# Three late modulation rows: features on partitions and a row sum on VectorE

## The chip, the cores and the metric

The kernel runs on one core of a Trainium2 chip. The metric is the device time of one execution in microseconds (us), lower is better. Of three runs the median was 1469.58 us (1468.6 to 1469.86).

## The reference, cut to what matters

One layer of a hybrid backbone: two adaLN modulated inputs (256 latent tokens `x`, 256 context tokens), one input projection, three mixers (S5, convolution, mLSTM), an output projection, then a SwiGLU FFN. Only this part of it is touched:

```python
def _adaln(c_vec, w_mod, b_mod):                # D_MODEL = 2048, w_mod (2048, 6*2048)
    m = jax.nn.silu(c_vec) @ w_mod + b_mod
    return jnp.split(m[..., None, :], 6, axis=-1)
sh1_x, sc1_x, g1_x, sh2_x, sc2_x, g2_x = _adaln(c, w_mod[l], b_mod[l])
x = x + g1_x * (jnp.concatenate([s5_x, cv_x, ml_x], axis=-1) @ w_out[l])
hx2 = _rmsnorm(x, norm2_g[l]) * (1.0 + sc2_x) + sh2_x
x = x + g2_x * _swiglu(hx2, w_ffn_in[l], w_ffn_out[l])
```

`sh1` and `sc1` are needed first and are formed elsewhere. The four later rows are called q = 0 (`g1`), 1 (`sh2`), 2 (`sc2`) and 3 (`g2`). Each is a product of a 2048 vector with a 2048 x 2048 fp32 matrix of 16 MB.

## The kernel before, in words

**The main stream.** All large weights lie in HBM in the order of use, as chunks of eight 128 x 128 tiles (512 KB). SP fetches chunk c into `raw` (L259, three buffers), ScalarE rounds it to `whi` (L201) and VectorE forms the rest `wlo = raw - whi` (L168). TensorE then runs three fp32r matmuls per tile (`mm3`, all recorded at L208), with 256 tokens as columns. `nxt()` hands out tiles and starts the fetch and the split one or two chunks ahead.

**The stages, by time in the profiled execution.** The first modulation rows and the first tiles of the input projection (to 150 us), the rest of the projection with convolution, S5 and k (to 350), v (to 443), q and o with attention (to 582), the gate of S5 and the output projection in two halves (to 691), the second norm and the first four FFN column blocks (`make_h2`, to 744), the FFN (to 1455), the final norm.

**The four late rows.** `wm_dma` (L331) loads pieces of 128 x 1024 fp32 (512 KB) on POOL's queue into four buffers `wm`; the first four before the job starts, and one more for each piece used. `mod_job` (L719) walks q, then four column blocks b of 512 features, then 8 pieces. For q = 0 TensorE multiplies each piece with the vector `cs`. For q = 1 to 3, the three rows that the change touches, the piece has model inputs on partitions: ScalarE writes the first scaled step into `macc` (L195), VectorE adds 15 further steps, each a SCALAR_TENSOR_TENSOR of 128 x 512 (L179) with one column of `cs` as its scalar. The sum over the 128 partitions is still open. Four TensorE transposes (L749) put the features on partitions and ScalarE adds each along its row (L755, with an accumulator read). `macc` has one buffer, so the next block cannot begin before L755 is through with it.

**What sets the order.** `Sched` is a planner with modelled clocks of TensorE, VectorE and ScalarE. Its `pump()`, called at every chunk, lets jobs emit code: a job that yields n waits n ns of modelled TensorE time, here 5000 for each piece (`MOD_PACE_D`; 4000 for q = 3), and nothing is emitted while the modelled VectorE or ScalarE is over 3500 ns ahead. `mst["go"]` holds q = 1 back until the k stage and q = 3 until the first FFN blocks are emitted. `need_mod(q)` emits what is left when a row is needed: q = 0 before the output projection, q = 2 after its first half (L1178), q = 3 before the first FFN output (L1274). The text order is then a priority only: when the program is built, a scheduler may put an instruction on its engine ahead of the text where its inputs and its buffer are free, unless the text pins it (`keep_in_program_order`, as for the ScalarE step of q = 3 at L738). On the chip every engine and every DMA queue takes its instructions in the order so fixed.

Of the kernel before, what the change touches and what calls it, by code (L numbers as in the profile page):

```python
# [10 lines left out]
F32 = mybir.dt.float32  # L11
F32R = mybir.dt.float32r
I32 = mybir.dt.int32
AF = mybir.ActivationFunctionType
OP = mybir.AluOpType
# [4 lines left out]
KT = 16  # L20
# [14 lines left out]
MOD_PACE = 3200.0  # L35
MOD_PACE_F = 4000.0
MOD_PACE_D = 5000.0
# [5 lines left out]
CONV_STEP = 2  # L43
GO_AT = {'k': 2}
LEAD_R, LEAD_S = 2, 1
MOD_PE = {(0, b) for b in range(4)}

# [98 lines left out]


@with_exitstack  # L150
def hybrid_layer_kernel(ctx: ExitStack, tc: tile.TileContext, xt, ctxt, wm1, wmr, wst, wg, bvrow, pvd, cstd, s5p, out):
    nc = tc.nc
    V, S, P, G = nc.vector, nc.scalar, nc.tensor, nc.gpsimd
    sb = ctx.enter_context(tc.tile_pool(name="sb", bufs=1))
# [3 lines left out]
    sc = Sched()  # L158


    def n_of(ap):
        n = 1
        for s in ap.shape[1:]:
            n *= s
        return n

    def tt(o, a, b, op):
        V.tensor_tensor(out=o, in0=a, in1=b, op=op)  # L168
        sc.dve += 62 + 1.05 * n_of(o)

    def ts(o, a, s1, op0, s2=None, op1=None):
        if op1 is None:
            V.tensor_scalar(o, a, s1, None, op0=op0)
        else:
            V.tensor_scalar(o, a, s1, s2, op0=op0, op1=op1)
        sc.dve += 62 + 0.6 * n_of(o)

    def stt(o, a, s, b, op0, op1):
        V.scalar_tensor_tensor(o, a, s, b, op0=op0, op1=op1)  # L179
        sc.dve += 62 + 1.05 * n_of(o)  # L180

    def vcopy(o, a):
# [3 lines left out]
    def rsum(o, a):  # L186
        V.tensor_reduce(out=o, in_=a, op=OP.add, axis=mybir.AxisListType.X)
        sc.dve += 62 + 1.05 * n_of(a)
# [5 lines left out]
    def act(o, a, f, bias=0.0, scale=1.0, pin=False):  # L194
        i = S.activation(o, a, f, bias=bias, scale=scale)  # L195
        if pin:
            tc.keep_in_program_order(i)
        sc.act += 190 + 0.84 * n_of(o)

    def acopy(o, a):  # L200
        S.copy(o, a)  # L201
        sc.act += 190 + 0.84 * n_of(o)

    def mm(o, l, r, start, stop, native=False, tp=None, sgc=False, pin=False):
        kw = {}
        if tp is not None:
            kw["tile_position"] = tp
        i = P.matmul(o, lhsT=l, rhs=r, start=start, stop=stop, skip_group_check=sgc, **kw)  # L208
        if pin:
            tc.keep_in_program_order(i)  # L210
        n = n_of(o)
        sc.pe += (max(n * 4, 512) if native else max(n, 256)) / 2.36 / (1 if tp is None else 4)

    def bank(tag, bufs, dt=F32):
        return pp.tile([128, 512], dt, name="ps_" + tag, tag=tag, bufs=bufs)

    def mbank():
        return bank("m", 3)

    def qbank():  # L220
        return bank("qk", 2)

    def bbank():
        return bank("b", 3)

    def tmp(n=512):
        return sb.tile([128, 512], F32, name="tmp", tag="tmp", bufs=4)[:, :n]
# [9 lines left out]
    def pvc(name, i=0, n=None):  # L237
        a, w = PV[name]
        return pv[:, a + i:a + i + (n if n is not None else 1)]
# [77 lines left out]
    wm = {}  # L317
# [7 lines left out]
    def wm_dma(key, src, q=None):  # L325
        slot = (4 * key[0] + key[1]) % NWX if len(key) == 2 else 0
        if slot < NWM:
            wm[key] = sb.tile([128, 1024], F32, name="wm", tag="wm", bufs=NWM)
        else:
            wm[key] = wm_extra[slot - NWM]  # L330
        i = (q or nc.gpsimd).dma_start(wm[key], src)  # L331
        if q is not None:
            tc.keep_in_program_order(i)
# [33 lines left out]

    plan_pump()

    cs = sb.tile([128, KT, 32], F32, name="cs")  # L370
    V.memset(cs, 0.0)
    act(cs[:, :, 0], pvc("c", 0, 16), AF.Silu)
    act(cs[:, :, 1], pvc("cc", 0, 16), AF.Silu)
    b1sc = sb.tile([128, 16], F32, name="b1sc")
    ts(b1sc, pvc("bm", 16, 16), 1.0, OP.add)

    hx = sb.tile([128, KT, 2, NT], F32R, name="hx", tag="hx")
# [29 lines left out]
    for half, src in ((0, xr), (1, cr)):  # L407
        for q in range(4):
# [4 lines left out]
            for i in range(2):  # L413
                mm(stp[:, half * 256:half * 256 + 256], ones, sq[:, 256 * i:256 * i + 256], q + i == 0, q + i == 4,
                   native=True)
# [288 lines left out]

    mods = sb.tile([128, 4, 16], F32, name="mods")

    mq = [(q, b, kp) for q in range(4) for b in range(4) for kp in range(8)]
    mst = {"d": 0, "q": 0, "go": 0}

    def phase(n):  # L710
# [2 lines left out]
    def mod_dma():  # L713
        if mst["d"] < len(mq):
            i = mq[mst["d"]]
            wm_dma(i, wmr[i[0], i[1], i[2]])
            mst["d"] += 1

    def mod_job():  # L719
      for q in range(4):  # L720
        while mst["go"] < q:
            yield 500
        for b in range(4):
            on_pe = (q, b) in MOD_PE
            acc = sb.tile([128, 512], F32, name="macc", tag="macc", bufs=1)
            if on_pe:
                psm = bbank()
            for kp in range(0, 8, 2):
                w = [wm.pop((q, b, kp + i)).rearrange("p (k n) -> p k n", k=2) for i in range(2)]
                for j in range(4):  # L730
                    kt = 2 * kp + j
                    wj = w[j // 2][:, j % 2, :]
                    s = cs[:, kt, 0:1]
                    if on_pe:
                        mm(psm[32 * j:32 * j + 32, :], cs[:, kt, :], wj, kt < 4, kt >= 12, native=True, tp=(0, 32 * j),
                           pin=j > 0)
                    elif kt == 0:
                        act(acc, wj, AF.Copy, scale=s, pin=q == 3)  # L738
                    else:
                        stt(acc, wj, s, acc, OP.mult, OP.add)  # L740
                mod_dma()
                mod_dma()
                yield 2 * (MOD_PACE if on_pe else MOD_PACE_D if q < 3 else MOD_PACE_F)
            dst = mods[:, q, 4 * b:4 * b + 4]
            if on_pe:
                acopy(acc, psm)
            ps = bbank()
            for j in range(4):
                P.transpose(ps[:, 128 * j:128 * j + 128], acc[:, 128 * j:128 * j + 128], ident)  # L749
                sc.pe += 110  # L750
            if on_pe:
                rsum(dst, ps.rearrange("p (f j r) -> p f j r", f=4, j=4)[:, :, :, 0])
            else:
                for j in range(4):
                    S.activation(acc[:, 128 * j:128 * j + 128], ps[:, 128 * j:128 * j + 128], AF.Copy,  # L755
                                    accum_out=dst[:, j:j + 1])
                    sc.act += 390
            tt(dst, dst, pvc("bm", 32 + 16 * q + 4 * b, 4), OP.add)
            yield
        mst["q"] = q + 1  # L760

    def need_mod(q):
        mst["go"] = max(mst["go"], q)
# [169 lines left out]
    for t in range(4):  # L933
        ps = mbank() if t else bbank()
# [68 lines left out]
    for ct in range(KHEAD, 8):  # L1003
        ps = mbank()
        for kt in range(KT):
            w = nxt()
# [116 lines left out]
    for ct in range(8):  # L1123
        ps = mbank()
# [3 lines left out]
    for ct in range(8):  # L1128
        ps = mbank()
# [31 lines left out]
    for ct in range(4):  # L1161
        ps = mbank()
        for kt in range(4):
            mm3(ps[:, 0:256], nxt(), (gs[:, kt, 0, :], gs[:, kt, 1, :]), kt == 0, kt == 3)
        sg, f = tmp(256), tmp(256)
# [5 lines left out]
    for ct in range(KT):  # L1171
        ps = mbank()
        for i in range(8):
            src, j = (mx["c"], i) if i < 4 else (mixs, i - 4)
# [38 lines left out]
    for ct in range(KT):  # L1213
        ps = mbank()
# [32 lines left out]
    def ffn_in(b):  # L1247
        ffa = (ffp if b % 2 else sb).tile([128, FBLK, 2, NT], F32R, name="ffa", tag="fb" if b % 2 else "hx")
        ffas[b] = ffa
        i0 = 0  # L1250
        if b == 0:
            pss = [mbank(), mbank(), mbank(), qbank()]
            for kt in range(KT):
                make_h2(kt)
                hh = (h2[:, kt, 0, :], h2[:, kt, 1, :])
                for i in range(FHEAD):
                    mm3(pss[i][:, 0:256], nxt(), hh, kt == 0, kt == KT - 1, sgc=True)
                    mm3(pss[i][:, 256:512], nxt(), hh, False, kt == KT - 1, sgc=True)
            for i in range(FHEAD):
                swiglu(ffa, i, pss[i])  # L1260
            i0 = FHEAD
            mst["go"] = 3
        for i in range(i0, FBLK):
            ps = bbank() if b == 0 and i < FHEAD + 2 else mbank()
            fourA(1, h2, ps[:, 0:256])
            fourA(1, h2, ps[:, 256:512])
            swiglu(ffa, i, ps)

    s3 = None
    for kind, b in FSEQ:  # L1270
# [8 lines left out]
        for ct in range(KT):  # L1279
            ps = mbank()  # L1280
# [13 lines left out]
    i = 0  # L1294
# [8 lines left out]
def pack(inp):  # L1303
    f = {k: np.asarray(v) for k, v in inp.items()}
# [7 lines left out]
    a = {}  # L1312
    a["xt"] = feat(f["x"][0])
    a["ctxt"] = feat(f["ctx"][0])
    wmod = f["w_mod"][0]
    m1 = wmod[:, :4096].reshape(4, 4, 128, 2, KT, 128)
    a["wm1"] = np.ascontiguousarray(m1.transpose(4, 0, 2, 1, 3, 5)).reshape(KT, 4, 128, 1024)
    mr = wmod[:, 4096:].reshape(8, 2, 128, 4, 4, 512)
    a["wmr"] = np.ascontiguousarray(mr.transpose(3, 4, 0, 2, 1, 5)).reshape(4, 4, 8, 128, 1024)
    mats = {"in": f["w_in"][0][:, :OFF_G], "out": f["w_out"][0], "glu": f["s5_w_glu"][0], "ffi": f["w_ffn_in"][0],  # L1320
            "ffo": f["w_ffn_out"][0]}
    til = {k: m.reshape(m.shape[0] // 128, 128, m.shape[1] // 128, 128) for k, m in mats.items()}
    w = np.empty((NCH, 128, CH, 128), np.float32)
# [49 lines left out]
    for r in range(32):  # L1373
        q = r % 16
# [9 lines left out]
    return a  # L1384


_INS = ["xt", "ctxt", "wm1", "wmr", "wst", "wg", "bvrow", "pvd", "cstd", "s5p"]


# [19 lines left out]
```

## Time and profile before

| | us |
|---|---|
| median of three runs | 1469.58 |
| the profiled execution, device time | 1469.76 |
| its span, first to last instruction | 1468.0 |
| TensorE busy | 1423.0 (97%) |
| VectorE busy | 1004.2 (68%) |
| ScalarE busy | 716.0 (49%) |
| bytes moved by DMA | 315.56 MB, mean 215 GB/s |

The device time is 1.76 us more than the span. An engine that is busy for most of the span may still wait for another one in some stage, so the rows below go by stage. A matmul's shown duration overlaps the next one's; the distance between starts is what a matmul takes of the time.

### The profile page before, as it was taken

To read this page: it belongs to the slowest core of one execution; us is meant where nothing else is said; L and a number is where in the kernel's file an instruction comes from. 1 tells how busy PE (TensorE), PEld (TensorE's weight loads), DVE (VectorE), ACT (ScalarE), POOL (GpSimd) and SP (SyncE) were. 2 spreads that over 40 slices of the span, in tenths; PEclk is the share of its full clock that TensorE was granted. 3 is DMA by queue.
4 is the path that set the end of the run, shared out by engine and by line. 5 is a ranking of instruction groups with operands and counts; after the bars stand their busy time and mean duration, and the time that the engine had idled before them with its cause. 6 is when DMAs were issued, how large, how long until landed. Compare 5 with 4: busy or idle time off the path is not lost.

```text
span 1468.0 us, 29243 instructions
## 1 busy us (share of the span) xinstructions
PE 1423.0 (97%) x11840; PEld 1335.7 (91%) x11840; DVE 1004.2 (68%) x1960; ACT 716.0 (49%) x1199; POOL 107.2 (7%) x207
## 2 busy tenths in 40 slices
PE   6999899999999999998999999999999999999996
PEld 3888788887878999998999999999999999999996
DVE  7655699998988787988776667555544554555554
ACT  4333786654656555545544444433444334443353
POOL 1221111110101011111010000000000000000000
PEclk9999999999999999999999999999999999999999
DMA  9997464443436576688477786555555555555553
GB/s 359 360 360 294 160 234 138 165 162 123 147 121 233 196 270 237 239 312 321 150 262 269 257 291 237 186 187 187 185 184 185 186 188 182 186 187 187 186 175 114
DMA packets 87943, 315.56 MB, mean 215 GB/s; under 512 B 10096, under 2 KB 10880, under 8 KB 87808
## 3 DMA queue, kind: packets, MB, share of 16 engines
q1 hardware_dynamic: 60912, 216.67, 42.9%
q0 software_dynamic: 26896, 97.02, 18.4%
q8 instruction: 93, 1.52, 0.4%
q14 instruction: 42, 0.34, 0.1%
HBM read 311.55 MB, written 2.10 MB: 214 GB/s over the span
## 4 chain that ended last, share of the span: by engine, by line
PE 87%; DVE 4%; ACT 3%; DMA 2%; issue 2%; SPq 0%; POOL 0%; DVEq 0%; POOLq 0%; ACTq 0%
PE ps_m L208 71%; PE ps_b L208 11%; PE ps_qk L208 4%; DMA wm<-in_wm_dram 1%; DVE tmp L168 1%; DMA tmp<-in_wg_dram 1%; DVE macc L179 1%; DMA raw<-in_wst_dram 1%; DVE wlo L168 1%; PE ps_b L839 0%; ACT whi L201 0%; ACT tmp L195 0%; ACT U L201 0%; PE ps_b L749 0%; DVE xres L168 0%
## 5 line engine op out<-in xcount | busy, mean ns | idle before, releaser
L168 DVE TENSOR_TENSOR wlo<-raw,whi 128x1024 fp32r<-128x1024 f32 x386 | 471.9, 1224 | 315.9 <-ACT whi L201 311.1
L201 ACT CAST whi<-raw 128x1024 fp32r<-128x1024 f32 x386 | 404.0, 1047 | 502.3 <-PE ps_m L208 355.9
L208 PE MATMUL ps_m<-h,whi 128*128 128x256 f32 x2624 | 469.9, 282 | 3.6 <-ACT h L195 3.6
L208 PEld LDWEIGHTS ps_m<-h,whi 128*128 128x128 f32 x2624 | 403.8, 189 | 4.0 <-ACT h L195 4.0
L208 PE MATMUL ps_m<-h,wlo 128*128 128x256 f32 x1312 | 369.6, 282 | 0.0
L208 PE MATMUL ps_m<-ffa,whi 128*128 128x256 f32 x1408 | 251.1, 281 | 0.0
L208 PEld LDWEIGHTS ps_m<-h,wlo 128*128 128x128 f32 x1312 | 247.5, 189 | 0.0
L208 PEld LDWEIGHTS ps_m<-ffa,whi 128*128 128x128 f32 x1408 | 215.7, 188 | 1.4 <-issue 1.2
L208 PE MATMUL ps_m<-ffa,wlo 128*128 128x256 f32 x704 | 197.3, 280 | 0.0
L208 PE MATMUL ps_m<-hx,whi 128*128 128x256 f32 x960 | 186.9, 290 | 5.5 <-ACT hx L195 3.6
L208 PEld LDWEIGHTS ps_m<-hx,whi 128*128 128x128 f32 x960 | 148.8, 190 | 24.7 <-issue 16.3
L179 DVE SCALAR_TENSOR_TENSOR macc<-wm,cs,macc 128x512 f32<-128x512 f32 x180 | 134.6, 748 | 6.8 <-ACT macc L195 5.1
L208 PE MATMUL ps_m<-hx,wlo 128*128 128x256 f32 x480 | 135.5, 283 | 0.4 <-DVE wlo L168 0.4
L208 PEld LDWEIGHTS ps_m<-ffa,wlo 128*128 128x128 f32 x704 | 132.2, 188 | 0.0
L331 POOL DMA_DIRECT2D wm<-in_wmr_dram x128 | 67.5, 528 | 606.8 <-DVE macc L179 429.8
L208 PEld LDWEIGHTS ps_m<-hx,wlo 128*128 128x128 f32 x480 | 90.9, 190 | 0.8 <-DVE wlo L168 0.8
L179 DVE SCALAR_TENSOR_TENSOR xres<-ps_m,mods,xres 128x256 f32<-128x256 f32 x96 | 46.1, 482 | 35.2 <-PE ps_m L208 35.0
L179 DVE SCALAR_TENSOR_TENSOR XB<-XB,pv 128x256 f32<-128x256 f32 x120 | 53.9, 481 | 0.6
L208 PE MATMUL ps_m<-hc,whi 128*128 128x256 f32 x256 | 52.9, 288 | 0.0
L208 PE MATMUL ps_m<-mixm,whi 128*128 128x256 f32 x256 | 47.0, 285 | 0.0
L208 PE MATMUL ps_m<-whi,hx 128*128 128x512 f32 x128 | 46.5, 400 | 0.0
L201 ACT CAST ffa<-tmp 128x256 fp32r<-128x256 f32 x44 | 17.7, 405 | 49.7 <-DVE tmp L168 49.7
(267 smaller groups left out, 1967.2 us busy)
## 6 DMA issues: line engine op xcount, KB each, us to landing
raw<-in_wst_dram SPq DMA_DIRECT2D x386, 512.0 KB, 3.5
wm<-in_wmr_dram POOLq DMA_DIRECT2D x128, 512.0 KB, 5.4
wm<-in_wm_dram POOLq DMA_DIRECT2D x32, 512.0 KB, 7.2
wmu<-in_wm_dram POOLq DMA_DIRECT2D x16, 512.0 KB, 7.2
wmt<-in_wm_dram POOLq DMA_DIRECT2D x7, 512.0 KB, 5.9
wm<-in_wm_dram SPq DMA_DIRECT2D x5, 512.0 KB, 10.2
xr<-in_xt_dram SPq DMA_DIRECT2D x4, 512.0 KB, 6.5
cr<-in_ctxt_dram SPq DMA_DIRECT2D x4, 512.0 KB, 9.0
```

The costliest lines, as they stand in the source:

```text
L168: V.tensor_tensor(out=o, in0=a, in1=b, op=op)
L179: V.scalar_tensor_tensor(o, a, s, b, op0=op0, op1=op1)
L201: S.copy(o, a)
L208: i = P.matmul(o, lhsT=l, rhs=r, start=start, stop=stop, skip_group_check=sgc, **kw)
L331: i = (q or nc.gpsimd).dma_start(wm[key], src)
```

## The change

For q = 1 to 3 the matrix is stored transposed in HBM. A piece now holds 128 features on partitions and 1024 model inputs along the row. The vector `silu(c)`, 1024 of its values at a time, is spread over all partitions as `cbr`: a DMA on POOL's queue from one 4 KB row, then a Silu on ScalarE in place. One SCALAR_TENSOR_TENSOR of 128 x 1024 multiplies piece and `cbr`, writes the product over the piece and the sum along the row into one column of `mods` through `accum_out`. A feature has two halves of the vector, so each row takes 32 of these. The halves are visited as q1, q2 with the first half, q1, q2, q3 with the second, then q3 with the first, so `cbr` is loaded three times, into one buffer that it shares with `cs`. The sums of the second half visited go to `part`, and two small adds per row put halves and bias together. `macc`, L749 and L755 remain only as q = 0 needs them (its copy goes to `tmp`). The bytes of the matrices and their number of pieces stay. The gate `go = 3` is gone: q = 3 follows q = 2 at its own pace, and nothing in it is pinned.

```diff
-    def stt(o, a, s, b, op0, op1):
-        V.scalar_tensor_tensor(o, a, s, b, op0=op0, op1=op1)
+    def stt(o, a, s, b, op0, op1, accum=None):
+        V.scalar_tensor_tensor(o, a, s, b, op0=op0, op1=op1, accum_out=accum)
...
-    mq = [(q, b, kp) for q in range(4) for b in range(4) for kp in range(8)]
+    mq = [(0, b, kp) for b in range(4) for kp in range(8)]
+    mq += [(q, hf, i) for hf, qs in ((0, (1, 2)), (1, (1, 2, 3)), (0, (3,))) for q in qs for i in range(KT)]
...
-                    elif kt == 0:
-                        act(acc, wj, AF.Copy, scale=s, pin=q == 3)
-                    else:
-                        stt(acc, wj, s, acc, OP.mult, OP.add)
...
-            else:
-                for j in range(4):
-                    S.activation(acc[:, 128 * j:128 * j + 128], ps[:, 128 * j:128 * j + 128], AF.Copy,
-                                    accum_out=dst[:, j:j + 1])
...
+        mst["q"] = 1
+        while mst["go"] < 1:
+            yield 500
+        at, cbr, part = None, None, None
+        for q, hf, i in mq[32:]:
+            if hf != at:
+                at, cbr = hf, sb.tile([128, 1024], F32, name="cbr", tag="cs")
+                nc.gpsimd.dma_start(cbr, crow[0:1, 1024 * hf:1024 * hf + 1024].to_broadcast([128, 1024]))
+                yield 4000
+                act(cbr, cbr, AF.Silu)
+                yield 2000
+            second = hf == (q < 3)
+            if second and i == 0:
+                part = sb.tile([128, KT], F32, name="mpart", tag="b1sc")
+            w = wm.pop((q, hf, i))
+            stt(w, w, 1.0, cbr, OP.mult, OP.mult, part[:, i:i + 1] if second else mods[:, q, i:i + 1])
+            mod_dma()
+            if second and i == KT - 1:
+                tt(part, part, pvc("bm", 32 + 16 * q, KT), OP.add)
+                tt(mods[:, q], mods[:, q], part, OP.add)
+                mst["q"] = q + 1
+            yield MOD_PACE_D if q < 3 else MOD_PACE_F
...
-            mst["go"] = 3
```

## Rows read from the trace of the kernel before

**Rows 1.** The page: the chain that ended last, shares by engine.
```profile
PE 87%; DVE 4%; ACT 3%; DMA 2%; issue 2%; SPq 0%; POOL 0%; DVEq 0%; POOLq 0%; ACTq 0%
```
**Rows 2.** Busy time by stretch: us, engines (instructions), granted clock, DMA share, GB/s.
```profile
350.00:450.00 100.00, 98.93 (x656) 80.54 (x655) 84.95 (x218) 63.81 (x143) 8.50 (x16) 1.00 0.41 139
450.00:590.00 140.00, 135.62 (x964) 126.85 (x965) 110.90 (x246) 75.95 (x144) 14.24 (x27) 1.00 0.68 239
590.00:640.00 50.00, 49.16 (x410) 48.51 (x411) 44.69 (x72) 24.62 (x41) 4.22 (x8) 1.00 0.73 261
640.00:690.00 50.00, 49.67 (x419) 47.62 (x418) 45.61 (x65) 27.54 (x59) 8.45 (x16) 1.00 0.91 332
690.00:745.00 55.00, 50.50 (x408) 49.69 (x408) 38.51 (x72) 29.27 (x41) 0.00 (x0) 0.97 0.49 163
...
935.00:1400.00 465.00, 465.00 (x3926) 465.00 (x3925) 240.49 (x262) 186.87 (x216) 0.00 (x0) 1.00 0.56 186
```
**Rows 3.** All that touches `macc`: duration ns min/median/max, first and last start.
```profile
L179 DVE SCALAR_TENSOR_TENSOR macc<-wm,cs,macc x180: 718/748/757, 358.0 to 903.6; 128x512 f32<-128x512 f32 x180
...
L749 PE MATMUL ps_b<-cst,macc x64: 270/272/329, 203.0 to 928.3; 128*128 128x128 f32 x64
L755 ACT ACTIVATE macc<-ps_b x48: 258/278/294, 428.5 to 930.0; 128x128 f32<-128x128 f32 x48
L755 ACT ACTIVATION_READ_ACCUMULATOR macc<-ps_b x48: 193/210/228, 428.6 to 930.2; 128x1 f32 x48
L195 ACT ACTIVATE macc<-wm,cs x12: 708/724/753, 357.3 to 884.4; 128x512 f32<-128x512 f32 x12
```
**Rows 4.** The chain in order of time, around transposes: start, us, what.
```profile
640.20 0.44 PE ps_b L749 x4
```
**Rows 5.** The same chain in the FFN, its longest pieces.
```profile
836.54 45.57 PE ps_m L208 x384
882.55 45.56 PE ps_m L208 x384
```
**Rows 6.** VectorE groups by shape: busy us, mean ns of one, idle before.
```profile
L168 DVE TENSOR_TENSOR wlo<-raw,whi 128x1024 fp32r<-128x1024 f32 x386 | 471.9, 1224 | 315.9 <-ACT whi L201 311.1 <-PE ps_b L208 3.0
...
L179 DVE SCALAR_TENSOR_TENSOR XB<-XB,pv 128x256 f32<-128x256 f32 x120 | 53.9, 481 | 0.6
...
L168 DVE TENSOR_TENSOR dn<-dn,ps_b 128x1 f32<-128x1 f32 x16 | 2.4, 149 | 0.2
```
**Rows 7.** VectorE in order of time, output projection: start, us, what.
```profile
671.55 0.74 DVE L179 SCALAR_TENSOR_TENSOR macc<-wm,cs,macc 128x512 f32<-128x512 f32 x1
672.21 1.22 DVE L168 TENSOR_TENSOR wlo<-raw,whi 128x1024 fp32r<-128x1024 f32 x1
673.35 0.74 DVE L179 SCALAR_TENSOR_TENSOR macc<-wm,cs,macc 128x512 f32<-128x512 f32 x1
```
**Rows 8.** POOL in order of time: transfers issued for one block and the next.
```profile
568.71 0.53 POOL L331 DMA_DIRECT2D wm<-in_wmr_dram  x1 [30.12 <-DVE macc L179]
571.30 0.53 POOL L331 DMA_DIRECT2D wm<-in_wmr_dram  x1 [2.06 <-DVE macc L179]
...
588.20 0.53 POOL L331 DMA_DIRECT2D wm<-in_wmr_dram  x1 [4.23 <-DVE macc L179]
607.29 0.53 POOL L331 DMA_DIRECT2D wm<-in_wmr_dram  x1 [18.56 <-DVE macc L179]
```
**Rows 9.** VectorE in order of time while the second norm is applied.
```profile
703.51 0.42 DVE L168 TENSOR_TENSOR h<-tmp,h 128x256 fp32r<-128x256 f32 x1
703.85 0.41 DVE L175 TENSOR_SCALAR tmp<-tmp,A,mods 128x256 f32<-128x256 f32 x1
...
721.23 0.76 DVE L168 TENSOR_TENSOR h<-tmp,h 128x256 fp32r<-128x256 f32 x2
...
725.20 1.23 DVE L168 TENSOR_TENSOR wlo<-raw,whi 128x1024 fp32r<-128x1024 f32 x1 [1.62 <-ACT whi L201]
```
**Rows 10.** DMA issues: KB each, median us to landing.
```profile
wm<-in_wmr_dram POOLq DMA_DIRECT2D x128, 512.0 KB, 5.4
...
bvb<-in_bvrow_dram SPq DMA_DIRECT2D x2, 256.0 KB, 3.7
```
**Rows 11.** ScalarE groups by shape.
```profile
L201 ACT CAST whi<-raw 128x1024 fp32r<-128x1024 f32 x386 | 404.0, 1047 | 502.3 <-PE ps_m L208 355.9 <-DMA raw<-in_wst_dram 54.3 <-PE ps_qk L208 39.8
L195 ACT ACT_TABLE_LOAD x25 | 32.1, 1283 | 3.7 <-DMA pv<-in_pvd_dram 3.3
...
L195 ACT ACTIVATE U<-U 128x1024 f32<-128x1024 f32 x1 | 1.1, 1062 | 0.5 <-DVE U L179 0.5
```

More of the change, by code (lines that the diff above doesn't have):

```diff
@@ L45 @@
 LEAD_R, LEAD_S = 2, 1
-MOD_PE = {(0, b) for b in range(4)}
 def tile_order():
@@ L150, in hybrid_layer_kernel @@
 @with_exitstack
-def hybrid_layer_kernel(ctx: ExitStack, tc: tile.TileContext, xt, ctxt, wm1, wmr, wst, wg, bvrow, pvd, cstd, s5p, out):
+def hybrid_layer_kernel(ctx: ExitStack, tc: tile.TileContext, xt, ctxt, wm1, wmg, wmr, wst, wg, bvrow, crow, pvd, cstd,
+                        s5p, out):
     nc = tc.nc
@@ L368, in hybrid_layer_kernel @@
     plan_pump()
-    cs = sb.tile([128, KT, 32], F32, name="cs")
+    cs = sb.tile([128, KT, 32], F32, name="cs", tag="cs")
     V.memset(cs, 0.0)
@@ L373, in hybrid_layer_kernel @@
     act(cs[:, :, 1], pvc("cc", 0, 16), AF.Silu)
-    b1sc = sb.tile([128, 16], F32, name="b1sc")
+    b1sc = sb.tile([128, 16], F32, name="b1sc", tag="b1sc")
     ts(b1sc, pvc("bm", 16, 16), 1.0, OP.add)
@@ L715, in mod_dma @@
             i = mq[mst["d"]]
-            wm_dma(i, wmr[i[0], i[1], i[2]])
+            wm_dma(i, wmg[i[1], i[2]] if i[0] == 0 else wmr[i[0] - 1, i[2], i[1]])
             mst["d"] += 1
     def mod_job():
-      for q in range(4):
-        while mst["go"] < q:
-            yield 500
         for b in range(4):
[L724 to L727, printed above, removed]
+            psm = bbank()
             for kp in range(0, 8, 2):
-                w = [wm.pop((q, b, kp + i)).rearrange("p (k n) -> p k n", k=2) for i in range(2)]
+                w = [wm.pop((0, b, kp + i)).rearrange("p (k n) -> p k n", k=2) for i in range(2)]
                 for j in range(4):
                     kt = 2 * kp + j
[L732 to L736, printed above, removed]
-                    elif kt == 0:
-                        act(acc, wj, AF.Copy, scale=s, pin=q == 3)
-                    else:
-                        stt(acc, wj, s, acc, OP.mult, OP.add)
+                    mm(psm[32 * j:32 * j + 32, :], cs[:, kt, :], w[j // 2][:, j % 2, :], kt < 4, kt >= 12, native=True,
+                       tp=(0, 32 * j), pin=j > 0)
                 mod_dma()
                 mod_dma()
[L743 to L746, printed above, removed]
+                yield 2 * MOD_PACE
+            acc = tmp()
+            acopy(acc, psm)
             ps = bbank()
@@ L750, in mod_job @@
                 sc.pe += 110
-            if on_pe:
-                rsum(dst, ps.rearrange("p (f j r) -> p f j r", f=4, j=4)[:, :, :, 0])
-            else:
-                for j in range(4):
-                    S.activation(acc[:, 128 * j:128 * j + 128], ps[:, 128 * j:128 * j + 128], AF.Copy,
-                                    accum_out=dst[:, j:j + 1])
-                    sc.act += 390
-            tt(dst, dst, pvc("bm", 32 + 16 * q + 4 * b, 4), OP.add)
-            yield
-        mst["q"] = q + 1
+            dst = mods[:, 0, 4 * b:4 * b + 4]
+            rsum(dst, ps.rearrange("p (f j r) -> p f j r", f=4, j=4)[:, :, :, 0])
+            tt(dst, dst, pvc("bm", 32 + 4 * b, 4), OP.add)
+            yield
+        mst["q"] = 1
[20 more added lines that the diff above has]
+            yield MOD_PACE_D if q < 3 else MOD_PACE_F
     def need_mod(q):
@@ L1317, in pack @@
     a["wm1"] = np.ascontiguousarray(m1.transpose(4, 0, 2, 1, 3, 5)).reshape(KT, 4, 128, 1024)
-    mr = wmod[:, 4096:].reshape(8, 2, 128, 4, 4, 512)
-    a["wmr"] = np.ascontiguousarray(mr.transpose(3, 4, 0, 2, 1, 5)).reshape(4, 4, 8, 128, 1024)
+    mg = wmod[:, 4096:6144].reshape(8, 2, 128, 4, 512)
+    a["wmg"] = np.ascontiguousarray(mg.transpose(3, 0, 2, 1, 4)).reshape(4, 8, 128, 1024)
+    a["wmr"] = np.ascontiguousarray(wmod[:, 6144:].T.reshape(3, KT, 128, 2, 1024).transpose(0, 1, 3, 2, 4))
+    a["crow"] = np.ascontiguousarray(f["c"][0:1])
     mats = {"in": f["w_in"][0][:, :OFF_G], "out": f["w_out"][0], "glu": f["s5_w_glu"][0], "ffi": f["w_ffn_in"][0],
@@ L1384, in pack @@
     return a
-_INS = ["xt", "ctxt", "wm1", "wmr", "wst", "wg", "bvrow", "pvd", "cstd", "s5p"]
+_INS = ["xt", "ctxt", "wm1", "wmg", "wmr", "wst", "wg", "bvrow", "crow", "pvd", "cstd", "s5p"]
 def kernel(**inputs):
```

## Prediction

> **What bounds the kernel now.** I read the chain that ended last first: TensorE holds 87% of it, the other engines 3 or 4% each [rows 1]. Next the busy times by stretch, to see where TensorE waits. From 350 us, where the changed rows begin, the stretch's length less TensorE's busy time gives 1.07, 4.38, 0.84, 0.33 and 4.50 us of idle time up to 745, 11.1 us in all, and none from 935 to 1400 [rows 2]. So nearly all of the time is matmuls that stand in line. Work on VectorE, ScalarE or the queues counts only where it makes one of them late; work on TensorE counts in full. VectorE is the nearest to being late: busy 286.2 of the 340 us from 350 to 690, with 53.9 us to spare, against 240.5 of 465 in the FFN [rows 2].
>
> **TensorE, what goes.** Each of the 12 blocks (three rows of four) ends in four transposes. In the FFN a chain piece of 45.57 us begins at 836.54, the next at 882.55: 0.44 us lies between, and that is such a block [rows 5]. The chain shows the same 0.44 us for the block at 640.20 [rows 4]. The others lie where TensorE is busy for about 97% or more [rows 2], so 12 x 0.44 = 5.28 us leave the path. Nothing on TensorE is added. This is the one term of the sum that needs no cover.
>
> **VectorE, what is exchanged.** Out go 180 steps of 128 x 512. One lasts 748 ns [rows 3], but the next instruction begins 0.66 us after it [rows 7], so they occupy 180 x 0.66 = 118.8 us. In come 96 steps of 128 x 1024 with a row sum. From 256 to 512 elements the operation goes from 481 to 748 ns [rows 3, 6], 1.043 ns for an element; 512 more make 1282 ns, and less the same 0.09 us of overlap 1.19 us (the subtraction of `wlo`, also 128 x 1024, takes 1224 ns and hands on after 1.14 [rows 6, 7]). The trace has no row sum on VectorE. From below it costs nothing; from above I take ScalarE's accumulator read, 0.21 us [rows 3]; I take 0.06 us, a 128 x 1 operation of VectorE (149 ns [rows 6]) less the overlap, since that is the same engine. That makes 96 x 1.25 = 120 us, between 114 and 134: an even exchange. The 12 small adds of the bias become 6. If the cover fails, 15 us more would still lie within the 53.9 us to spare, so I put nothing into the sum.
>
> A row that speaks for the full rate: the step with two fp32 inputs from SBUF already runs at 1.04 ns an element, no slower than the plain subtraction. [...]
>
> **ScalarE.** Out go 48 pairs of row sum and accumulator read (278 and 210 ns) and 12 first steps (724 ns) [rows 3]: 48 x 0.49 + 12 x 0.72 = 32 us of instruction time. In come three Silu over 128 x 1024, 1.06 us as the nearest row has it, each with a load of its function table of 1.28 us and perhaps one back [rows 11]: 3.6 us a time, 11 in all. Behind such a Silu on ScalarE stands the next rounding to `whi`, and behind that `wlo` and TensorE. A chunk of 24 matmuls lasts 45.57/384 x 24 = 2.85 us [rows 5]; three `whi` buffers let a rounding begin two chunks before its use, 5.7 us, of which it and `wlo` need 1.05 and 1.14 [rows 7, 11]. So 3.5 us of delay are hidden and 3.6 nearly. If ScalarE also has to wait for the row to land, each of the three could cost up to about 3 us: 0 to 9, and I take 0, as the text puts the Silu 4 us of modelled time behind its DMA.
>
> **Queues.** The weights' bytes stay. `cbr` adds three transfers of 512 KB on POOL's queue; the nearest, a row spread to 256 KB, lands after 3.7 us, a piece after 5.4 [rows 10]. Each waits until VectorE has finished with the `cbr` before it, and while it and the Silu run no step can: about 5.4 + 2.3 = 8 us of pause, twice within the stream (the first falls in front of it). On POOL's queue only later pieces stand behind it, and the small loads of S5; on SP's nothing is moved.
>
> **Order, where the larger effect may lie.** A block's eight transfers start from 568.71 to 588.20, some 2.8 us apart where the planner asks for 5 us, and the next block's begin only at 607.29; `macc` is what POOL waits for [rows 8]. So steps run ahead of the text until `macc` stops them. Without `macc` only the four buffers and `cbr` hold them, and I expect one stream without those gaps: it needs 120 us of VectorE, and has 118.8 x 2/3 + 53.9 = 133 us up to 690, so q = 2 should be ready well before the second norm and q = 3 shortly before or after it. That fills VectorE from 350 to 690 to over 90%. In the stretch 640 to 690 it is at 45.6 of 50 already, with DMA at 332 GB/s, and TensorE lost 0.33 us [rows 2]. Hence I charge only 0.7 us, half a step now and then in front of something urgent, between 0 and the 4 us below.
>
> **Sum.** The profiled execution took 1469.76 us, 0.18 above the median. 1469.76 - 5.28 + 0.7 = 1465.2, and against the median 1465.0.
>
> **The rivals.**
>
> *More is given back.* Of the 11.1 us idle time, 4.5 belong to the second norm's chain, which stays. If the other 6.6 also go, as transposes and row sums no longer stand in the queues of TensorE and ScalarE, it is 1465.0 - 0.7 - 6.6 = 1457.7. Against it: they end on waits that have other causes too, such as S5 at 350 to 450. Chance 0.10, for 1457.5 to 1463.
>
> *q = 3 crowds the second norm* (no change). Up to about 722 VectorE has no gap there, and from 725 it waits 1.62 us in each chunk [rows 9]. Three operations of 0.34 us for each of 16 columns [rows 9] and 16 times 1.14 make 34 of the 45.6 us that TensorE needs for this stage. If the stream is late, steps come at 4 us each, 11.4 in this time, 14.3 us: 3 us too many, and one more step of 1.25 us before the norm's first result. Then it is 1465.0 - 0.7 + 4.2 = 1468.5. It decides from about ten steps left at 697. The removed gate held back just these. Chance 0.20, for 1467 to 1471.
>
> *The weights come late* (slower). In the FFN the weights alone take 186 GB/s [rows 2]; one piece per chunk, 0.524 MB in 2.85 us, would add 184. 370 is more than the 332 of rows 2, and with equal shares the weights would get 166 of 186: 11% slower as long as it lasts, 11 us for 100 us, up to 1475. [...] Against it: in the 50 us at 332 GB/s hardly anything was lost, and S5, attention and the swaps of `cbr` thin the stream. Chance 0.10, for 1470 to 1478.
>
> [...] Chance 0.06.
>
> *The late row is late.* If the swaps keep q = 2 from being ready at about 690, each us is one us of idle TensorE. A pause of 8 us that nothing hides gives 1473, but the first swap lies far ahead of 690 and only the lag that is left of it counts. Chance 0.04, for 1469 to 1476.
>
> **How the numbers follow.** My forecast, 1463 to 1467, has 0.50. A change within 0.2% (2.9 us) can't be told from none here. Faster, below 1466.6, are nearly all of the forecast (0.47), the first rival (0.10) and 0.01 of the second: 0.58. The same are the rest of the forecast (0.03), 0.17 of the second and 0.01 of the last: 0.21. Slower is the remainder, 0.21. The range 1460 to 1473 leaves out the half rate, half of the late weights and the ends of the first and last rival, some 0.17.
>
> **What would show it.** Right: L749 only 16 times, all for q = 0; FFN pieces of the chain without 0.44 us breaks; the new step at 1.2 to 1.4 us; POOL's transfers without gaps of 18 to 30 us but for the swaps, the last step before 760 us in place of 903.6 [rows 3]; TensorE idle 9 to 12 us between 350 and 745. Wrong: a step over 2 us; ScalarE waiting for `cbr`; more than 15 us idle between 350 and 745; VectorE with steps between 697 and 722 and TensorE waiting for `h2`; roundings that wait for `raw` for clearly more than the 54.3 us of before [rows 11].

## The result and the profile after

The changed kernel takes 1491.76 us (median of 4 runs, 1486.81 to 1493.33), the kernel before on the same chip 1469.09 (4 runs, 1467.32 to 1469.86): 1.0150 times as long, 95% interval 1.0125 to 1.0176. The forecast was 1465. The profiled execution of the changed kernel took 1493.33 us, its span is 1491.6; against the one of before that is 23.6 us more.

First the exchange itself: all that touches the spread row `cbr` in the changed kernel, and by line the transposes that are left (columns as in [rows 3]):

```profile
L179 DVE SCALAR_TENSOR_TENSOR wm<-wm,cbr x96: 1190/1217/1226, 340.2 to 654.0; 128x1024 f32<-128x1024 f32 x96
L179 DVE DVE_READ_ACCUMULATOR wm<-wm,cbr x96: 75/81/90, 341.3 to 655.1; 128x1 f32 x96
L750 POOL DMA_DIRECT2D cbr<-in_crow_dram x3: 527/527/530, 321.7 to 591.3; - x3
L195 ACT ACTIVATE cbr<-cbr x3: 1050/1056/1061, 328.6 to 601.9; 128x1024 f32<-128x1024 f32 x3
```

```profile
L736 PE MATMUL ps_b<-cst,tmp x16: 272/273/473, 206.8 to 390.2; 128*128 128x128 f32 x16
```

A step lasts 1217 ns with its row sum and is followed by an accumulator read of 81 ns. The transposes of three rows are gone. The steps begin at 340 us instead of 358 and end at 654 instead of 904 [rows 3]. In the FFN one chain piece now runs over the places where [rows 5] have their 0.44 us: 

```profile
819.92 140.16 PE ps_m L208 x1168
```

(140.16 us for 1168 matmuls are 120.0 ns each; [rows 5] have 45.57 for 384, 118.7 ns. The last section comes back to this.)

Then the stretches (columns as in [rows 2]) and TensorE's waits from 340 to 760 us (line waited for: us in total, times, longest):

```profile
350.00:450.00 100.00, 91.68 (x542) 73.04 (x540) 91.74 (x221) 49.29 (x109) 16.44 (x32) 0.93 0.65 226
450.00:590.00 140.00, 136.00 (x979) 125.98 (x979) 132.32 (x321) 75.61 (x134) 24.80 (x47) 1.00 0.85 297
590.00:640.00 50.00, 41.47 (x303) 40.40 (x302) 38.51 (x65) 24.36 (x35) 5.80 (x11) 0.86 0.70 249
640.00:690.00 50.00, 50.00 (x428) 48.91 (x428) 36.17 (x52) 21.34 (x27) 1.58 (x3) 1.00 0.67 227
690.00:745.00 55.00, 50.51 (x399) 49.00 (x399) 40.16 (x74) 29.06 (x43) 0.00 (x0) 0.94 0.46 151
```

```profile
PE ps_b L736 <- ACT tmp L201: 6.5, 1, 6.5
PE ps_m L208 <- ACT RH L195: 5.4, 1, 5.4
PE ps_m L208 <- ACT h L195: 3.5, 1, 3.5
```

TensorE idles 25.3 us between 350 and 745, where it idled 11.1 [rows 2]. And the granted clock of two stretches fell, from 1.00 to 0.93 over 100 us and to 0.86 over 50 us. As an estimate from these rows that is 100 x 0.07 + 50 x 0.14 = 14 us of full speed, and with the 14.2 us of added idle time 28 us (some of it counted twice, where TensorE idled at the low clock). That is about the 23.6 us of loss and the 5.3 us that were to be saved. Up to 745 us the loss lies in two places, 350 to 450 and 590 to 640. A further part of the 23.6, some 4.7 us, are the slower matmuls of this one execution in the FFN (last section). With them the parts make some 33 us where 28.9 are to be explained, so they are sizes and not an exact sum.

**At 340 to 400 us** the convolution's layer norm ends. VectorE there (start, us, what):

```profile
382.80 0.42 DVE L168 TENSOR_TENSOR tmp<-XB,tmp 128x256 f32<-128x256 f32 x1
383.13 1.22 DVE L179 SCALAR_TENSOR_TENSOR wm<-wm,cbr 128x1024 f32<-128x1024 f32 x1
384.28 0.08 DVE L179 DVE_READ_ACCUMULATOR wm<-wm,cbr 128x1 f32 x1
384.28 0.42 DVE L168 TENSOR_TENSOR mixc<-tmp,mixc 128x256 fp32r<-128x256 f32 x1
384.62 1.22 DVE L179 SCALAR_TENSOR_TENSOR wm<-wm,cbr 128x1024 f32<-128x1024 f32 x1
```

Between two short operations that hand on after 0.34 us stands a step of 1.14 us. From 340 to 390 us 24 steps run, 27 us of VectorE's time; before, there were 13 of half the size, 8.6 us. They stand first between the last steps of the convolution (`XB`), then in one serial chain, the layer norm and `mixc`. The larger part of the delay is there before the norm begins, as the last `XB` steps show, before the change and after it:

```profile
344.62 4.65 DVE L179 SCALAR_TENSOR_TENSOR XB<-XB,pv 128x256 f32<-128x256 f32 x9
```

```profile
363.37 0.48 DVE L179 SCALAR_TENSOR_TENSOR XB<-XB,pv 128x256 f32<-128x256 f32 x1
```

They end at 349.27 and at 363.85, 14.6 us apart; the last `mixc` ends 19.7 us later than before. Inside the norm the kernel before also had steps between the links, of 0.66 us each. The first row's fourth copy out of PSUM needs one of the four `tmp` buffers that this chain holds, and TensorE's transposes stand in line behind the copy. On ScalarE and TensorE (in square brackets the idle time before, and what ended it), and the granted clock of the two stretches around it:

```profile
388.92 0.56 ACT L201 COPY tmp<-ps_b 128x512 f32<-128x512 f32 x1
...
389.54 1.11 PE L736 MATMUL ps_b<-cst,tmp 128*128 128x128 f32 x4 [6.52 <-ACT tmp L201]
```

```profile
380.00:390.00 10.00, 3.48 (x15) 2.57 (x15) 10.00 (x21) 5.62 (x10) 2.82 (x6) 0.85 1.00 371
390.00:400.00 10.00, 9.15 (x63) 7.25 (x61) 6.61 (x20) 4.89 (x14) 0.87 (x2) 0.50 0.47 162
```

In the ten microseconds behind the 6.52 us of idling the granted clock is at 0.50; from 401 to 410 us it is at 1.00. Behind the 5.40 us of idling at the second place below it is at 0.50 as well, from 603.4 to 608.4, and at 1.00 from 609 to 620. That the idling is what lowers it is the author's reading of these two places; no run shows what sets the clock.

**At 590 to 640 us** it is the third fetch of the row. ScalarE in order of time, and TensorE's wait:

```profile
600.64 1.28 ACT L195 ACT_TABLE_LOAD   x1 [4.57 <-DMA cbr<-in_crow_dram]
601.94 1.06 ACT L195 ACTIVATE cbr<-cbr 128x1024 f32<-128x1024 f32 x1
602.90 0.46 ACT L195 ACTIVATE RH<-ps_m,pv 128x256 f32<-128x256 f32 x1
603.26 1.03 ACT L201 CAST whi<-raw 128x1024 fp32r<-128x1024 f32 x1
604.31 1.28 ACT L195 ACT_TABLE_LOAD   x1
605.60 1.91 ACT L195 ACTIVATE RH<-RH 128x2048 f32<-128x2048 f32 x1
...
603.41 0.79 PE L208 MATMUL ps_m<-gs,whi 128*128 128x256 f32 x2 [5.40 <-ACT RH L195]
```

ScalarE waits 4.57 us for the row to land, loads a table and forms the Silu. Behind that stands the last readout of the o projection out of PSUM into `RH` (602.90), and TensorE, which waits 5.40 us, goes on as soon as it is done, at 603.41. A rounding and the sigmoid over the whole of that `RH` with its table load come later still.

### The profile page after: what moved, and what is told of

It is laid out like the page before. It is cut to its first block, busy times and chain, and to the rows that moved or that the text cites. A ratio compares the mean times of both kernels' runs of the same rounds, so it can differ in the third digit from the quotient of the medians.

```text
span 1491.6 us, 28960 instructions
## 1 busy us (share of the span) xinstructions
PE 1430.9 (96%) x11792; PEld 1343.0 (90%) x11792; DVE 988.4 (66%) x1966; ACT 699.7 (47%) x1096; POOL 108.8 (7%) x210
## 4 chain that ended last, share of the span: by engine, by line
PE 78%; issue 9%; DVE 6%; ACT 2%; DMA 2%; POOL 2%; SPq 0%; POOLq 0%; DVEq 0%; ACTq 0%
PE ps_m L208 65%; PE ps_b L208 10%; PE ps_qk L208 3%; POOL wm L331 2%; DVE tmp L168 1%; DVE wm L179 1%; DMA tmp<-in_wg_dram 1%; DMA cbr<-in_crow_dram 1%; DVE wlo L168 1%; ACT tmp L195 1%; DVE XB L179 0%; ACT U L201 0%; PE ps_b L843 0%; DVE tmp L191 0%; ACT whi L201 0%
## 5 line engine op out<-in xcount | busy, mean ns | idle before, releaser
L208 PE MATMUL ps_m<-h,wlo 128*128 128x256 f32 x1312 | 373.4, 285 | 0.0
L179 DVE SCALAR_TENSOR_TENSOR wm<-wm,cbr 128x1024 f32<-128x1024 f32 x96 | 116.1, 1216 | 8.5 <-ACT cbr L195 5.9
L331 POOL DMA_DIRECT2D wm<-in_wmr_dram x96 | 50.6, 528 | 264.6 <-DVE wm L179 187.6
```

Of the source, the lines that this page charges most:

```text
L179: V.scalar_tensor_tensor(o, a, s, b, op0=op0, op1=op1, accum_out=accum)
```

## The experiments

Each experiment is compared with the kernel before on its own chip; that kernel's medians lay between 1467.9 and 1468.6. Times in us are medians; the ratios, with their 95% intervals, go by all executions, and a kernel's distance to the one before can differ by some 2 us between the two. "Lag" is the start of the `wlo` subtraction of weight chunk c less its start in the kernel before, from the two profiled executions. The changed kernel's lag is 0.4 us at chunk 45 (349 us), 13.0 at chunk 65 (472), 19.6 at 95 (605) and 23.6 at 280. In the expectations T is the theory that the `tmp` buffer of the first row's copies is a cause by itself, O or V that the steps' place in VectorE's order is, D that the weight loads crowd each other.

**The first loss: buffer or early steps.** Four runs: the copies back in a buffer of their own; the 96 steps held where the text writes them; both; and the kernel before with only the copies moved to `tmp`.

```diff
-            acc = tmp()
+            acc = csm[:, 512:1024]       # cs = csm[:, 0:512], one tile with tag "cs"
...
+        if accum is not None:
+            tc.keep_in_program_order(i)  # i = the step
...
-            acc = sb.tile([128, 512], F32, name="macc", tag="macc", bufs=1)
+            acc = tmp() if on_pe else sb.tile([128, 512], F32, name="macc", tag="macc", bufs=1)
```

> The changed kernel, with the first row's four copies out of PSUM going to 2 KB of their own (the unused half of the cs tile) instead of a tmp buffer. Theory T (the tmp buffer): the fourth copy can go ahead of the conv layer norm again, the 6.5 us TensorE wait at 389.5 us goes, and with it the half clock behind it; 1492 falls by 8 to 13 us, to 1479 to 1484. Theory O (the steps' place: a step needs only its weights and the row, so it goes ahead of conv and norm work on VectorE): the conv end stays late, and the time stays within 3 us of 1492.

> The changed kernel, with the 96 steps held at the place in VectorE's order where the text writes them (the last then at chunk 193 instead of 105). Theory O: the losses at 340-400, 470-490 and 590-625 us mostly go, the time falls by 12 us or more, to 1480 or less. Theory T: the 6.5 us wait at 389.5 us stays, so at least 8 us of the loss stay (1478 or more), and if the steps' place had no part at all it stays near 1492.

> Both edits of the two runs beside it. Theories T and O together: the conv end as early as before the change, no wait for the copy, steps spread to chunk 193; what is left is the 48 transposes saved (about 5 us) against three fetches of the spread row with a Silu and table loads: 1464 to 1470. If a third cause (the fetches of the row, the weights' new shape) has a large part, it stays above 1475.

> The kernel before, with only the first row's four copies out of PSUM moved from macc to a tmp buffer; the other three rows as before. Theory T: the fourth copy comes late by conv's tmp buffers, TensorE waits some 6 us at about 385 us and loses clock behind it: 1469 rises by 6 to 12 us, to 1475 to 1481. Theory O: no change, within 2 us of 1469.

Measured: own buffer 1481.40 us (ratio to before 1.0082, interval 1.0059 to 1.0105); steps held 1497.82 (1.0200, 1.0178 to 1.0222); both 1498.17 (1.0208, 1.0192 to 1.0223); before with `tmp` 1476.04 (1.0051, 1.0035 to 1.0068). By the numbers alone T had won both of its tests, and the run with both edits, expected at 1464 to 1470, took 1498. But the traces say otherwise on T. In the kernel before with `tmp` there is no wait for the copy; TensorE loses its time at 453 us, and the reason is another order on VectorE, where S5's copies now stand ahead of a split:

```profile
445.38 4.55 DVE L183 COPY gT<-U 32x128 f32<-32x128 f32 x16
...
453.17 0.58 PE L208 MATMUL ps_m<-hx,wlo 128*128 128x256 f32 x1 [6.99 <-DVE wlo L168]
```

And with the steps held the copies still go through `tmp`, yet its lag at chunk 65 is -1.4 us, with its own buffer -1.5: no loss at all in this place. The own buffer had also shifted the steps, since it lies in the tile into which the row is fetched: only 6 instead of 24 run before 390. A run that undoes only the early start settles it:

```diff
+            # in the loop over (q, half, i), for stt():
+                held=q == 1 and hf == 0)     # keep_in_program_order for these 16 steps
```

> The changed kernel as it is, first row's copies in tmp and all, with only the first 16 of the 96 steps held at the place where the text writes them (chunks 47 to 60 instead of 44 to 49). The run with its own buffer had also moved the first steps back, from 340 to 360 us, since the copy sits in the tile that the row is fetched into. If the early steps make conv late and the tmp buffer only passes that on, this run gains the same: 1492 falls to 1478 to 1484 and the 6.5 us wait goes. If the buffer is the cause, the wait stays and so does the time (over 1487).

Measured: 1479.11 us (1.0075, 1.0058 to 1.0092), 12.7 us less than the changed kernel (11.0 by the ratios). Five steps run before 390 us, the last `XB` step ends at 348.65, the copy into `tmp` comes at 366.78 instead of 388.92, TensorE no longer waits for it, and the lag at chunk 65 is -3.0 us instead of 13.0. The early steps are the cause here; the buffer only passes their delay on to TensorE. Two things stay open. The edit also moves what follows (the last step from 654 to 693 us), so of the 16.0 us that this place shows in the two profiled executions, 12.7 are left at the end. And no run has the early steps without `tmp`, so whether they would reach TensorE by another way as well isn't shown.

Why the runs with all steps held are the slowest is in their VectorE order before the second norm (steps held and own buffer, from 661 us; below it the stretch, columns as in [rows 2]):

```profile
661.85 1.22 DVE L179 SCALAR_TENSOR_TENSOR wm<-wm,cbr 128x1024 f32<-128x1024 f32 x1
...
663.00 1.22 DVE L179 SCALAR_TENSOR_TENSOR wm<-wm,cbr 128x1024 f32<-128x1024 f32 x1
...
664.14 1.22 DVE L179 SCALAR_TENSOR_TENSOR wm<-wm,cbr 128x1024 f32<-128x1024 f32 x1
...
665.29 1.22 DVE L168 TENSOR_TENSOR wlo<-raw,whi 128x1024 fp32r<-128x1024 f32 x1
...
668.61 1.23 DVE L179 SCALAR_TENSOR_TENSOR wm<-wm,cbr 128x1024 f32<-128x1024 f32 x1 [0.96 <-DMA wm<-in_wmr_dram]
```

```profile
640.00:690.00 50.00, 37.26 (x240) 33.05 (x238) 40.23 (x65) 12.57 (x16) 11.61 (x22) 0.83 0.91 317
```

At the planner's pace row 2 isn't done when `need_mod(2)` wants it, so the rest is written out in one bunch, some four steps to a chunk. Held there, they wait for their own weights with the splits of the stream behind them. TensorE idles 12.7 of 50 us, and the lag jumps from 6 to 33 us between chunks 95 and 115.

**The rest of the loss: loads, the third fetch, the place, the sum.** Four runs start from the run with its own buffer (1481.4): later loads cut to an eighth; no row sum; two fetches of the row by another order of the halves; two fetches and small loads.

```diff
-                nc.gpsimd.dma_start(wm[key], src)
+                nc.gpsimd.dma_start(t[:, 0:128], src[:, 0:128])   # t: one of four fixed tiles
...
-            stt(w, w, 1.0, cbr, OP.mult, OP.mult, part[:, i:i + 1] if second else mods[:, q, i:i + 1])
+            stt(w, w, 1.0, cbr, OP.mult, OP.mult)
...
-    mq += [(q, hf, i) for hf, qs in ((0, (1, 2)), (1, (1, 2, 3)), (0, (3,))) for q in qs for i in range(KT)]
+    mq += [(q, hf, i) for hf, qs in ((0, (1, 2, 3)), (1, (1, 2, 3))) for q in qs for i in range(KT)]
```

> The run with its own buffer, but after the first four loads of the three rows each later load brings only 128 of a tile's 1,024 columns, into the same four tiles (64 KB for 512 KB; the rest of the weights is left out, and a step multiplies by 0.25 so that values stay small). All 96 steps run at nearly the same places of VectorE's order. Theory D (the loads, now 440 to 690 us instead of spread to 900, crowd the weight stream: the raw loads of 5 to 7 us in the chain): most of what is left above the kernel before goes, 1481 falls to 1464 to 1470. Theory V (the steps themselves, ahead of casts and norms on VectorE): 1481 stays within 4 us.

> The run with its own buffer, with the 96 steps forming the product but no sum along the row (the sums are left out, their places set to zero). If the sum sets the step's price (the rival of a halved rate), a step falls from 1.2 to 0.7 us or less and the time falls by 3 us or more; our theory: the step stays at 1.14 to 1.22 us and the time within 3 us of 1481.

> The run with its own buffer, with the halves of the three rows visited in an order that needs two fetches of the spread row instead of three (first half of rows 1, 2, 3, then second half of 1, 2, 3): one fetch of 512 KB, one Silu and its table loads less, at about 590 to 650 us. If the third fetch is a cause of its own, 1481 falls by 3 us or more; if it is only one load among many, it stays within 2 us.

> Own buffer, two fetches of the row, and an eighth of each later weight load (the rest left out, steps times 0.25): both edits that gained 8.3 and 6.6 us alone. If the third fetch hurts only as one more transfer in the crowd, the two gains overlap and the time stays at 1472 to 1474; if it hurts by what it does on ScalarE and POOL, they add and the time falls to 1465 to 1468.

Measured: small loads 1473.13 us (1.0048, 1.0028 to 1.0068); no row sum 1480.40 (1.0081, 1.0062 to 1.0099); two fetches 1474.76 (1.0041, 1.0027 to 1.0056); both 1466.42 (0.9987, 0.9977 to 0.9996). The row sum costs nothing that can be told from zero: without it a step takes the same 1217 ns,

```profile
L179 DVE SCALAR_TENSOR_TENSOR wm<-wm,cbr x96: 1189/1217/1226, 359.6 to 685.7; 128x1024 f32<-128x1024 f32 x96
```

and the run is 1 us from the one with it. Loads (8.3 us) and third fetch (6.6 us) are two causes: together they gain 15.0, about their sum. By the ratios it is 5.0, 6.0 and 13.9 us, so the share of the loads is the less certain one; it fell between what D and what V foresaw. For the loads, the DMA issues from 440 to 700 us, in the run with its own buffer and in that with small loads (columns as in [rows 10]):

```profile
wm<-in_wmr_dram POOLq DMA_DIRECT2D x75, 512.0 KB, 5.6
raw<-in_wst_dram SPq DMA_DIRECT2D x64, 512.0 KB, 5.5
```

```profile
raw<-in_wst_dram SPq DMA_DIRECT2D x67, 512.0 KB, 3.6
wm<-in_wmr_dram POOLq DMA_DIRECT2D x75, 64.0 KB, 2.6
```

In the same time the kernel before issues 53 pieces, with 5.0 us for a `raw` load. So the run with small loads takes away more than the change had added, and no run makes the loads of the kernel before small. In the paced kernel below the same edit gains little or nothing (1463.87 us against 1463.46; 2.6 us by the ratios): most of what a full load costs, it costs in this order of the steps. For the third fetch, ScalarE waits 5.63 us for `cbr` at 644 us in the run with its own buffer, and three roundings stand behind it. The first and second fetch fall where little is urgent: with two fetches ScalarE's one wait for the row inside the stream is 1.80 us, at 535.

**What the transposes are worth, and a kernel that keeps it.** The kernel before without its 48 transposes; and a paced kernel: own buffer, steps held, pace 2,500 instead of 5,000 so that rows 1 and 2 stand evenly at chunks 47 to 98, row 3 behind a gate. Four variants of it: 48 transposes of a constant put back, no gate, copies in `tmp`, small loads.

```diff
-MOD_PACE_D = 5000.0
+MOD_PACE_D = 2500.0
...
+            while q == 3 and mst["go"] < 3:
+                yield 500
...
+            if i % 8 == 7:
+                ps = bbank()
+                for j in range(4):
+                    tc.keep_in_program_order(P.transpose(ps[:, 128 * j:128 * j + 128], ident, ident))
```

> The kernel before without the 48 transposes of rows 1 to 3: ScalarE sums the untransposed accumulator by rows instead, as often and in the same shape (that is not the reference's row). It sizes the saving alone. By the sum of the prediction the 12 places on TensorE's path return 0.44 us each: 1469 less 5.3, that is 1463 to 1465; if other work fills the places, within 2 us of 1469.

> Own buffer, steps held at the place where the text writes them, the pace number of rows 1 and 2 halved from 5,000 to 2,500 so that their 64 steps stand between chunks 47 and 98 instead of being bunched at 107 to 114 in front of the second norm, and row 3 held back to chunks 140 to 205 by the gate that the change took out. If the bunch made the loss of the pinned runs, the 23 us step at chunks 105 to 115 goes: 1498 falls to 1468 to 1478. Theory D keeps the denser loads of chunks 47 to 98 as a cost of 3 to 8 us above 1464; theory V alone gives 1464 to 1468.

> The paced kernel with 48 transposes of a constant put back on TensorE, four after every eighth step (held at their place; nobody reads what they write). It sizes the saving where the order of the steps is fixed. By the prediction's 0.44 us for a place of four, 1463.5 rises by 5.3 us to 1468 to 1470; if other work fills the places, it stays within 2 us of 1463.5.

> The paced kernel without the gate on row 3, whose 32 steps then stand at chunks 99 to 164 instead of 140 to 205, and the third fetch of the row at chunk 134. If the pace of rows 1 and 2 is what mattered, the time stays within 2 us of 1463.5; if row 3's steps and loads in front of the second norm (chunks 99 to 129) cost something, it rises by 3 us or more.

> The paced kernel with the first row's copies back in a tmp buffer, as in the changed kernel. If the tmp buffer costs its 8 to 10 us whatever the steps do, 1463.5 rises to 1471 to 1474; if it costs only where VectorE's steps make conv's layer norm late (the pinned pair showed no difference), it stays within 2 us.

> The paced kernel with an eighth of each later weight load. If the loads at the paced rate still crowd the weight stream, 1463.5 falls by 3 us or more; if pacing has taken that cost away, it stays within 2 us.

Measured (us, ratio to before and its 95% interval):

| kernel | median | lowest to highest | ratio | interval |
|---|---|---|---|---|
| before, no transposes | 1470.99 | 1468.70 to 1475.87 | 1.0022 | 1.0011 to 1.0034 |
| paced | 1463.46 | 1463.00 to 1470.54 | 0.9979 | 0.9965 to 0.9992 |
| paced, 48 transposes | 1470.11 | 1467.57 to 1473.53 | 1.0011 | 1.0001 to 1.0022 |
| paced, no gate | 1463.73 | 1462.25 to 1464.95 | 0.9964 | 0.9952 to 0.9976 |
| paced, `tmp` | 1465.43 | 1462.89 to 1471.34 | 0.9985 | 0.9973 to 0.9997 |
| paced, small loads | 1463.87 | 1460.56 to 1467.04 | 0.9961 | 0.9946 to 0.9975 |

The paced kernel is ahead of both, of the kernel before by 0.2% (without the gate by 0.4%), at the lower end of what theory V alone foresaw. With transposes put back at fixed places it loses 6.7 us (4.7 by the ratios), so the term of 5.3 was about right. Taken out of the kernel before they gain nothing: without TensorE in the loop a block is ready for the next sooner, and rows 1 and 2 are through by chunk 99 in the built order instead of 123. That the early steps and loads eat the saving (DMA share 0.86 from 450 to 590, where [rows 2] have 0.68) is a reading of this trace; no run takes it apart. The gate and the `tmp` buffer matter by some 2 us at most once the steps are spread, and the loads by 0 to 2.6. The stretches of the paced kernel without the gate, whose profiled execution took 1462.96 us:

```profile
350.00:450.00 100.00, 98.86 (x663) 81.40 (x662) 90.17 (x228) 62.73 (x135) 11.12 (x21) 1.00 0.54 170
450.00:590.00 140.00, 136.57 (x969) 127.31 (x968) 122.08 (x279) 76.44 (x124) 22.71 (x43) 1.00 0.85 301
590.00:640.00 50.00, 48.93 (x415) 48.34 (x415) 45.13 (x78) 21.33 (x28) 5.28 (x10) 1.00 0.77 273
```

Against the changed kernel DMA moves as much from 450 to 590, and VectorE is busy for 122 us where it was 132. TensorE is back to 98.86 of 100 us in the first stretch and to 48.93 of 50 in the third, at a granted clock of 1.00: what differs is where the steps stand, and with them the loads behind them and the third fetch, which is issued at 710 us here, in the FFN, instead of 591.

## Why the prediction was wrong

**TensorE, right.** The places of 0.44 us are gone, and where the order is fixed they are worth 6.7 us (4.7 by the ratios) against the 5.28 of the sum, within the scatter of these runs.

**VectorE, right.** The step lasts 1.22 us and hands on after 1.14, where 1.25 was taken; the next instruction begins together with the accumulator read, so the sum adds nothing. 96 x 1.14 = 109 us replace 118.8. No run shows the half rate that has a chance of 0.06 in the forecast: a step takes 1217 ns with the row sum and 1217 without, where the subtraction of that shape takes 1224 [rows 6].

**Order, the step that failed.** It foresaw that the steps run ahead of the text without `macc`, and charged "0.7 us, half a step now and then in front of something urgent", after looking for the harm in VectorE's total from 350 to 690 us and at the second norm. The total did suffice. The harm lay at the stream's start, which the prediction never looked at, in serial work of short operations, the last steps of the convolution above all and the layer norm behind them: with a step let in before a link, that link comes 1.14 us later, and 24 steps ran there by 390 us. Its end fed TensorE through a copy that the change had moved to `tmp`, a move to which the sum gave no term. In place of the 0.7 us this place alone measured 12.7 us: 6.5 of it the one wait, and about 5 what ten microseconds at half clock cost (an estimate from the stretch 390 to 400).

**ScalarE, a size inside its bounds.** The step took 0 of "0 to 9", as the text puts the Silu behind its DMA. But the third fetch took 9.3 us to land, and ScalarE waited for it. It measured 6.6 us, from one fetch of three. The tables were cheaper than its 3.6 us a time allowed for: the changed kernel has 27 table loads in all where [rows 11] have 25; the wait for the row was the larger part.

**Queues, and the weights that come late.** The sum put nothing on the weights' queue, since the bytes stay; the rival priced a stream of pieces against the FFN's weights, with equal shares for both. Those shares were the author's assumption, and no run shows how the queues share; what the runs show is a `raw` load that lands after 5.5 us (median, 440 to 700 us) among full loads and after 3.6 among small ones. The crowd was at 440 to 700 us, ahead of the FFN, and cost 8.3 us in the run where it was cut (5.0 by the ratios).

**The account.** 1491.8, less 12.7 (the early first steps) = 1479.1; or by the own buffer, which does the same by another way, 1481.4; less 15.0 (loads and third fetch) = 1466.4. The paced kernel, 1463.5, is no further step of that row, for it has the full loads and all three fetches. From the run with its own buffer it saves 17.9 us by the place of the steps, and of the loads and the third fetch with them; what the 2.9 beyond the 15.0 are isn't shown. That 1463.5 is near the 1465.0 predicted shows what the exchange can be worth, not that the forecast was right: the order had to be made. Not in this account are the slower matmuls of the last section: the changed kernel's profiled execution had them, and whether its others did is not known. Of the list of what would show it, the right signs all came but TensorE's idle time, and of the wrong ones ScalarE waiting for `cbr` and more than 15 us idle did; roundings waited less for `raw` than before (11.2 us in all). Open is which operations behind the dense loads lose the 8.3 us: ScalarE's waits for `raw` from 440 to 700 are 14.5 us in the run with its own buffer and 2.7 with small loads, but 23.1 in the kernel before, so that count alone does not explain it.

## What to carry to other kernels

A dependency that one takes out may have been the brake that kept background work in its place: ask what the work will run ahead of once it is free, and cost it link by link in each serial chain there, not by the engine's total. Give such work its place (held instructions, a pace that ends before the deadline), for held at a pace too slow it bunches up and costs as much. To size a saving, put the work back into a kernel whose order is fixed; removing it from one that is scheduled anew measures the new order too.

## What of the hardware was not expected

The matmuls of the FFN ran at two speeds with the granted clock at 1.00. From 960 to 1160 us, TensorE busy throughout, the profiled execution of the changed kernel holds 1669 matmuls, that of before 1689:

```profile
960.00:1160.00 200.00, 200.00 (x1669) 200.00 (x1668) 101.22 (x110) 79.47 (x94) 0.00 (x0) 1.00 0.56 183
```

```profile
960.00:1160.00 200.00, 200.00 (x1689) 200.00 (x1689) 102.38 (x111) 80.73 (x93) 0.00 (x0) 1.00 0.55 185
```

That is 1.2%. From 760 to 960 us the two counts are the same again, so over both stretches it is 40 matmuls at 118.4 ns, as an estimate 4.7 of the 23.6 us between these two executions. From 1200 to 1400 us both hold 1689. Two other profiled executions have it from 760 to 1160 us: that of the run without a row sum (1669 in each stretch, 1486.55 us) and that of the paced kernel with small loads (1669 and 1673, 1467.04 us). All three were the slowest of their kernel's executions. So it comes and goes within an execution, at a granted clock of 1.00; as each kernel has one trace, whether its other executions had it isn't shown, and part of the scatter of 4 to 7 us may be this. Its cause stays open.
